# Normalised rows from the ring "in", made by ScalarE alone, and an in-place residual in the channel mixer's second half

## The chip, the cores and the metric

One core of a Trainium2 chip runs the kernel. The metric is the device time of one execution in microseconds (us); the kernel before took 1898.01 us (median of three runs, 1887.8 to 1898.91). Engines are called as in the profile: PE is TensorE (matmuls; PEld its weight loads), DVE is VectorE, ACT is ScalarE, POOL is GpSimd, SP is SyncE. L12 is line 12 of the kernel that the profile belongs to.

## The reference

Two layers of a hybrid backbone over 256 latent and 256 context tokens of 1024 channels. Each layer runs a token mixer and a channel mixer, each on normalised and modulated rows, and each followed by a residual with a second norm:

```python
def _layernorm(x):
    xf = x.astype(F32)
    xc = xf - jnp.mean(xf, axis=-1, keepdims=True)
    var = jnp.mean(xc * xc, axis=-1, keepdims=True)
    return (xc * lax.rsqrt(var + LN_EPS)).astype(x.dtype)

def _modulate(x, shift, scale):
    return _layernorm(x) * (1.0 + scale) + shift

def _post_ln(x, g, b):
    return _layernorm(x) * g + b
...
        x_mid = _post_ln(alpha * x + ada[:, 2] * y, ln1_g[l], ln1_b[l])
...
        h2 = _modulate(x_mid, ada[:, 3], ada[:, 4])
        if l % 2 == 0:
            j = l // 2
            f = _swiglu(h2, ffd_wg[j], ffd_wu[j], ffd_wd[j])
...
        x = _post_ln(alpha * x_mid + ada[:, 5] * f, ln2_g[l], ln2_b[l])
```

The context tokens go through the same steps with a modulation of their own. Matmuls are made of three products of a high and a low part (hi, lo) of each operand.

## The kernel before, in words

The 512 tokens are four tiles of 128 rows; the kernel works on them in two pairs, s = 0 (tiles 0 and 1, the context) and s = 1 (tiles 2 and 3, the latent tokens). A tile of 128 x 1024 numbers is held as two tiles of 128 x 512. These come from rings: "in" has 16, "C" 13 and "B" 14 slots of 128 x 512 (L120), "sg" has 4 (L110); there are three PSUM banks PM for products and three PX for transposes. A slot is given out in the order in which the program asks, and the next tile to take it waits until the last reader of the one before is done. The instructions of each engine are put in order by a scheduler ahead of the run, by priorities and by these rings, so the ring from which a tile comes sets where the instructions on it stand in an engine's order.

The change bears on two places.

Place 1 is the output projection of layer 0, 638 to 705 us. For each pair, `load_x` (L1648) fetches the rows x by POOL's DMA queue into four "in" tiles, `times_alpha` (L1058, ACT) scales them, and `out_proj` runs four groups of 48 matmuls over `tok_group`. `add_residual` takes each group's product: L1039 (DVE) multiplies it by the gate, L1040 (POOL) adds x times alpha, L1041 (DVE) takes the statistics. `post_ln` closes the norm: aggregate (L237), power (L229 DVE, L230 POOL), then the upper half of the columns by ACT and POOL (L1048 nb, L1049, L1050, L1051), the lower half by DVE (L1053, L1054). Then `modulate` calls `normalise`: statistics again (L246), power again, nb (L358), and the normalised rows z of two halves, L360 on ACT and L361 on DVE. PE transposes z in blocks of 128 x 128 (L373) into PX; L379 (DVE, odd blocks) or L381 (ACT, even blocks) applies scale and shift into an sg tile, L382 (ACT) rounds it to its high part, and L383 (DVE) takes the low part. The channel mixer's first matmuls follow (L222 to L224), with their activation at L1107.

Place 2 is the second half of the channel mixer and the start of layer 1's token mixer, 1063 to 1126 us. In `ffn` the down projection is done in halves. In the second, for each pair, four groups of 60 matmuls run, `add_residual` writes into new "in" tiles xn and reads the residual from zs, `post_ln` closes the norm, and `after` saves the latent rows (L1700) and calls `modulate` for layer 1. Behind it in the program stands layer 1's mixer: its first projection with evacuations L528 (ACT) and L531 (DVE), and on POOL a block of memsets and small parameter loads (L541, L547, L466 to L482, L537 to L543) and two loads of a table (L740).

Weights are fetched by SP's queue and split by L215 (ACT, hi) and L216 (DVE, lo) ahead of their matmuls.

Of the kernel before, what the change touches and what calls it, by code (L numbers as in the profile page):

```python
# [14 lines left out]
AF = mybir.ActivationFunctionType  # L15
OP = mybir.AluOpType
# [17 lines left out]
C_ID, C_SEL, _, C_CC, C_SC, C_MF, C_MB, C_ROPE, C_ONE, C_END = (  # L34
    0, 128, 130, 130, 258, 386, 514, 642, 770, 898)
# [60 lines left out]
def hybrid_backbone(ctx: ExitStack, tc: tile.TileContext, A, out, dbg=None, stop=None):  # L96
    nc = tc.nc
# [27 lines left out]
    def tt(tag, dt=F32, n=512):  # L125
        t = S["main"].tile([128, 512], dt, name=tag, tag=tag, bufs=TAGS[tag])
        return t if n == 512 else t[:, :n]
# [16 lines left out]
    def sg():  # L144
        return spool.tile([128, 512], F32, name="sg")
# [96 lines left out]
    def ln_stats(x):  # L242

        st = ln_open(2)
        for i in range(2):
            nc.vector.bn_stats(st[:, i, :], x[i])  # L246
        return ln_close(st)
# [107 lines left out]
    def normalise(x):  # L355
        mu, rs = ln_stats(x)
        nb = cc(1, "nb", bufs=4)
        nc.vector.scalar_tensor_tensor(nb, mu, -1.0, rs, op0=OP.mult, op1=OP.mult)  # L358
        z = [tt("B") for _ in range(2)]
        nc.scalar.activation(z[0], x[0], AF.Identity, scale=rs, bias=nb)  # L360
        nc.vector.tensor_scalar(z[1], x[1], mu, rs, op0=OP.subtract, op1=OP.mult)  # L361
        return z

    def modulate(l, xs, n0, s, act):
# [670 lines left out]

    def add_residual(z, g, p, r, ax, st, quick=False):
        c = slice(256 * (g % 2), 256 * (g % 2) + 256)
        zc = z[g // 2][:, c]
        nc.vector.tensor_tensor(zc, p, r[g // 2][:, c], op=OP.mult)  # L1039
        (nc.vector if quick else nc.gpsimd).tensor_tensor(zc, zc, ax[g // 2][:, c], op=OP.add)  # L1040
        nc.vector.bn_stats(st[:, g, :], zc)  # L1041

    def post_ln(z, st, rows, quick=False):
        g, b = rows
        mu, rs = ln_close(st)
        if not quick:
            nb = cc(1, "nb", bufs=4)
            nc.vector.scalar_tensor_tensor(nb, mu, -1.0, rs, op0=OP.mult, op1=OP.mult)  # L1048
            nc.scalar.activation(z[1], z[1], AF.Identity, scale=rs, bias=nb)  # L1049
            nc.gpsimd.tensor_tensor(z[1], z[1], g[1], op=OP.mult)  # L1050
            nc.gpsimd.tensor_tensor(z[1], z[1], b[1], op=OP.add)  # L1051
        for i in range(2 if quick else 1):
            nc.vector.scalar_tensor_tensor(z[i], z[i], mu, g[i], op0=OP.subtract, op1=OP.mult)  # L1053
            nc.vector.scalar_tensor_tensor(z[i], z[i], rs, b[i], op0=OP.mult, op1=OP.add)  # L1054
# [40 lines left out]
    def ffn(act, xm, fill, plan, after):  # L1095

        wg, wu, wd = A["ffd_wg"][0], A["ffd_wu"][0], A["ffd_wd"][0]
        zs = {}
        hid = {}

        def up(fp, sl):
            sgs = [None, None]

            def ev_g(i, p):
                s = sg()
                sgs[i] = s
                nc.scalar.activation(s[:, sl], p[:, sl], AF.Silu)  # L1107

            def ev_u(i, p):
                s = sgs[i]  # L1110
                nc.vector.tensor_tensor(s[:, sl], s[:, sl], p[:, sl], op=OP.mult)
                if fp + i not in hid:
                    hid[fp + i] = (tt("B", F32R), tt("C", F32R))
                hi, lo = hid[fp + i]
                nc.scalar.activation(hi[:, sl], s[:, sl], AF.Copy)
                nc.vector.tensor_tensor(lo[:, sl], s[:, sl], hi[:, sl], op=OP.subtract)
            col_pair(wg, 128 * fp, act, ev_g, sl)
            col_pair(wu, 128 * fp, act, ev_u, sl)

        def take(at):  # L1120
            for _ in range(plan.count(chr(65 + at))):
                fill.pop(0)()
        for half, (f0, f1) in enumerate(((0, 12), (12, 22))):
            for fp in range(f0, f1, 2):
                if fp == 0:
                    for sl in (slice(0, 256), slice(256, 512)):
                        for f in (0, 2):
                            up(f, sl)
                elif fp > 2:
                    up(fp, slice(0, 512))  # L1130
                if fp == 4:
                    for t in range(4):
                        times_alpha(xm[t])
                take(fp // 2)
            n = f1 - f0
            hh = ([hid[f][0] for f in range(f0, f1)], [hid[f][1] for f in range(f0, f1)])
            if half == 0:
                rows = {j: load_row(S["adarows"][1, 0, j, :], "in") for j in range(2)}
                for t in range(4):
                    zs[t] = xm[t]  # L1140
                for g in range(4):
                    def ev(t, p):
                        c = slice(256 * (g % 2), 256 * (g % 2) + 256)
                        k = sg()[:, :256]
                        nc.vector.tensor_tensor(k, p, rows[0 if t >= 2 else 1][g // 2][:, c], op=OP.mult)
                        nc.gpsimd.tensor_tensor(zs[t][g // 2][:, c], zs[t][g // 2][:, c], k, op=OP.add)
                    tok_group(wd[128 * f0:128 * f1], 256 * g, hh, ev, range(4), kk=n)
                    take(11 + g)
        ln2 = load_row(A["ln2_g"][0], "B"), load_row(A["ln2_b"][0], "B")
        for s in range(2):  # L1150
            tiles = (2 * s, 2 * s + 1)
            st = {t: ln_open(4) for t in tiles}
            xn = {t: [tt("in") for _ in range(2)] for t in tiles}
            for g in range(4):
                tok_group(wd[128 * f0:128 * f1], 256 * g, hh,
                          lambda t, p: add_residual(xn[t], g, p, rows[1 - s], zs[t], st[t]), tiles, kk=n)
                take(15 + 4 * s + g)
            for t in tiles:
                post_ln(xn[t], st[t], ln2)
            after(s, xn)  # L1160

# [488 lines left out]
    with phase("main") as S["main"]:  # L1652
# [24 lines left out]
        with phase("ff") as ff, deeper(ff, 3, 1, 1):  # L1677
            ff.tile([128, 16], F32, name="shift")
            act = new_act()
            rows = load_row(A["ln1_g"][0], "B"), load_row(A["ln1_b"][0], "B")  # L1680
            xm = {}
            for s in range(2):
                ax = {t: times_alpha(load_x(t, nc.gpsimd)) for t in (2 * s, 2 * s + 1)}
# [9 lines left out]
            def after(s, x):  # L1693
                if not act2:
                    act2.extend(new_act())
                for t in x:
                    for i in range(2):
                        dump("x0", x[t][i], lambda o: o[128 * t:128 * t + 128, 512 * i:512 * i + 512])
                        if t >= 2:
                            nc.gpsimd.dma_start(xsave[t - 2, :, 512 * i:512 * i + 512], x[t][i])  # L1700
                modulate(1, x, 0, s, act2)
# [9 lines left out]
        ax = {}  # L1711
# [45 lines left out]
```

## Time and profile before

| | |
|---|---|
| runs, median (lowest to highest) | 1898.01 us (1887.8 to 1898.91) |
| the profiled execution, its own time | 1892.86 us |
| its span, first to last instruction | 1891.1 us |
| mean granted clock of PE | 0.963 |
| busy: PE, DVE, ACT, POOL | 94%, 67%, 44%, 27% of the span |

The profiled execution is one more execution, a little under the median of the others. Start times in the rows count from the start of its span. A row of a timeline shows when it began, for how long its engine was in it, and in brackets how long the engine had been idle before it and what ended that.

### The profile page before, as it was taken

To read this page: it belongs to the slowest core of one execution; us is meant where nothing else is said; L and a number is where in the kernel's file an instruction comes from. 1 tells how busy PE (TensorE), PEld (TensorE's weight loads), DVE (VectorE), ACT (ScalarE), POOL (GpSimd) and SP (SyncE) were. 2 spreads that over 40 slices of the span, in tenths; PEclk is the share of its full clock that TensorE was granted. 3 is DMA by queue.
4 is the path that set the end of the run, shared out by engine and by line. 5 is a ranking of instruction groups with operands and counts; after the bars stand their busy time and mean duration, and the time that the engine had idled before them with its cause. 6 is when DMAs were issued, how large, how long until landed. Compare 5 with 4: busy or idle time off the path is not lost. (4 is left out here: it accounts for less than half of the span.)

```text
span 1891.1 us, 29054 instructions
## 1 busy us (share of the span) xinstructions
PE 1771.9 (94%) x10742; PEld 1408.3 (74%) x10742; DVE 1262.8 (67%) x2063; ACT 828.0 (44%) x1406; POOL 511.4 (27%) x530
## 2 busy tenths in 40 slices
PE   6899989999999979999999989989989899999995
PEld 3777977888777969789788978978979557554831
DVE  5677668666465786767775976587777667754823
ACT  3454555434443464221222445475555255543621
POOL 2353546552112630103101640036513100001000
PEclk8898999999999989999999989999999799999998
DMA  8434421114222636445775644233436789969995
GB/s 306 137 92 129 127 90 45 56 56 128 73 68 89 218 94 212 156 153 160 233 231 179 186 143 123 84 94 97 141 116 214 260 315 393 382 209 392 392 369 202
DMA packets 243933, 337.85 MB, mean 179 GB/s; under 512 B 16008, under 2 KB 158864, under 8 KB 243784
## 3 DMA queue, kind: packets, MB, share of 16 engines
q1 hardware_dynamic: 235896, 318.86, 50.5%
q0 software_dynamic: 6128, 13.96, 2.4%
q10 hardware_dynamic: 1760, 3.09, 0.4%
q8 instruction: 87, 1.43, 0.3%
q14 instruction: 62, 0.51, 0.1%
HBM read 333.74 MB, written 2.12 MB: 178 GB/s over the span
## 5 line engine op out<-in xcount | busy, mean ns | idle before, releaser
L216 DVE TENSOR_TENSOR lo<-raw,hi 128x1024 fp32r<-128x1024 f32 (+1 forms) x370 | 454.6, 1235 | 170.8 <-ACT hi L215 167.8
L215 ACT ACTIVATE hi<-raw 128x1024 fp32r<-128x1024 f32 (+1 forms) x370 | 368.2, 1001 | 439.7 <-PE PM L224 164.6
L222 PE MATMUL PM<-H,hi 128*128 128x512 f32 (+1 forms) x1104 | 388.7, 355 | 6.5 <-ACT sg L1107 2.9
L223 PE MATMUL PM<-H,hi 128*128 128x512 f32 (+1 forms) x1104 | 386.8, 351 | 1.5 <-DVE H L383 1.4
L224 PE MATMUL PM<-H,lo 128*128 128x512 f32 (+1 forms) x1104 | 384.0, 351 | 0.0
L222 PEld LDWEIGHTS PM<-H,hi 128*128 128x128 f32 x1104 | 211.3, 192 | 43.5 <-issue 4.4
L223 PEld LDWEIGHTS PM<-H,hi 128*128 128x128 f32 x1104 | 211.5, 192 | 32.3 <-DVE H L383 2.3
L224 PEld LDWEIGHTS PM<-H,lo 128*128 128x128 f32 x1104 | 210.1, 191 | 31.3 <-issue 2.7
L331 DVE SCALAR_TENSOR_TENSOR ad<-raw,silu,ad 128x512 f32<-128x512 f32 x208 | 176.3, 867 | 33.9 <-issue 12.9
L222 PE MATMUL PM<-hi,H 128*128 128x256 f32 x432 | 127.2, 294 | 4.1 <-ACT in L528 4.1
L223 PE MATMUL PM<-lo,H 128*128 128x256 f32 x432 | 126.8, 294 | 1.9 <-DVE lo L216 1.9
L224 PE MATMUL PM<-hi,H 128*128 128x256 f32 x432 | 125.9, 292 | 0.0
L1023 POOL TENSOR_TENSOR B<-B,sg 128x512 f32<-128x512 f32 (+1 forms) x48 | 62.6, 1316 | 216.5 <-DVE sg L1022 199.7
L1514 POOL TENSOR_TENSOR yl<-sg,yh 128x512 fp32r<-128x512 f32 x17 | 24.3, 1430 | 316.3 <-ACT yh L1513 295.9
L808 POOL TENSOR_TENSOR C<-C,in 128x512 f32<-128x512 f32 (+1 forms) x64 | 82.5, 1313 | 75.0 <-ACT C L807 64.2
L222 PE MATMUL PM<-hi,B 128*128 128x256 f32 x352 | 98.6, 280 | 0.0
L224 PE MATMUL PM<-hi,C 128*128 128x256 f32 x352 | 98.1, 279 | 0.0
L223 PE MATMUL PM<-lo,B 128*128 128x256 f32 x352 | 98.0, 278 | 0.0
L1386 PE MATMUL PM<-raw,xs 128*64 128x512 f32 (+3 forms) x448 | 96.5, 566 | 0.0
L222 PEld LDWEIGHTS PM<-hi,H 128*128 128x128 f32 x432 | 86.3, 200 | 5.7 <-ACT in L528 4.3
L223 PEld LDWEIGHTS PM<-lo,H 128*128 128x128 f32 x432 | 86.4, 200 | 4.1 <-DVE lo L216 2.2
L224 PEld LDWEIGHTS PM<-hi,H 128*128 128x128 f32 x432 | 86.1, 199 | 0.8 <-issue 0.8
(440 smaller groups left out, 3555.8 us busy)
## 6 DMA issues: line engine op xcount, KB each, us to landing
raw<-in_w_ada_dram SPq DMA_DIRECT2D x80, 512.0 KB, 4.3
raw<-in_moe_wd_dram SPq DMA_DIRECT2D x80, 512.0 KB, 8.2
raw<-in_w_gate_dram SPq DMA_DIRECT2D x64, 512.0 KB, 3.7
raw<-in_moe_wg_dram SPq DMA_DIRECT2D x60, 512.0 KB, 8.5
raw<-in_moe_wu_dram SPq DMA_DIRECT2D x60, 512.0 KB, 10.0
raw<-in_w_in_dram SPq DMA_DIRECT2D x54, 512.0 KB, 3.7
raw<-in_ffd_wd_dram SPq DMA_DIRECT2D x28, 512.0 KB, 3.5
raw<-in_ffd_wg_dram SPq DMA_DIRECT2D x26, 512.0 KB, 4.3
```

Source lines behind the costliest of these rows:

```text
L215: nc.scalar.activation(h[:, :m], raw[:, :m], AF.Copy)
L216: (nc.vector if ahead else nc.gpsimd).tensor_tensor(l[:, :m], raw[:, :m], h[:, :m], op=OP.subtract)
L222: nc.tensor.matmul(o, ah, bh, start=start, stop=False, **kw)
L223: nc.tensor.matmul(o, ah, bl, start=False, stop=False, **kw)
L224: nc.tensor.matmul(o, al, bh, start=False, stop=stop, **kw)
L331: nc.vector.scalar_tensor_tensor(acc[j], part, sc, acc[j], op0=OP.mult, op1=OP.add)
L808: nc.gpsimd.tensor_tensor(E[:, xt], E[:, xt], X[:, xt], op=OP.mult)
L1023: nc.gpsimd.tensor_tensor(mixed[c][:, xt], mixed[c][:, xt], s[:, xt], op=OP.add)
L1386: nc.tensor.matmul(po[g, :w.shape[-1]], x[:, c, :], w, start=(c < k), stop=(c + k >= kk), tile_position=(0, g.start))
L1514: nc.gpsimd.tensor_tensor(yl, y, yh, op=OP.subtract)
```

## The change

`normalise` takes z from the ring "in" in place of "B", and ACT makes both halves; L361 on DVE is gone. In the second half of `ffn`, the sum of the residual is written in place into zs; the product of gate and PSUM then goes into half an sg tile, k, and the four "in" tiles xn of each pair are gone. Lines behind the change move by up to two: L1039, L1040 and L1041 become L1041, L1042 and L1043; L1050 and L1051 become L1052 and L1053; L1648 becomes L1649.

```diff
@@ normalise
-        z = [tt("B") for _ in range(2)]
-        nc.scalar.activation(z[0], x[0], AF.Identity, scale=rs, bias=nb)
-        nc.vector.tensor_scalar(z[1], x[1], mu, rs, op0=OP.subtract, op1=OP.mult)
+        z = [tt("in") for _ in range(2)]
+        for i in range(2):
+            nc.scalar.activation(z[i], x[i], AF.Identity, scale=rs, bias=nb)
         return z
@@ add_residual
-        zc = z[g // 2][:, c]
-        nc.vector.tensor_tensor(zc, p, r[g // 2][:, c], op=OP.mult)
-        (nc.vector if quick else nc.gpsimd).tensor_tensor(zc, zc, ax[g // 2][:, c], op=OP.add)
+        zc, k = z[g // 2][:, c], z[g // 2][:, c]
+        if z is ax:
+            k = sg()[:, :256]
+        nc.vector.tensor_tensor(k, p, r[g // 2][:, c], op=OP.mult)
+        (nc.vector if quick else nc.gpsimd).tensor_tensor(zc, k, ax[g // 2][:, c], op=OP.add)
         nc.vector.bn_stats(st[:, g, :], zc)
@@ ffn
-            xn = {t: [tt("in") for _ in range(2)] for t in tiles}
             for g in range(4):
                 tok_group(wd[128 * f0:128 * f1], 256 * g, hh,
-                          lambda t, p: add_residual(xn[t], g, p, rows[1 - s], zs[t], st[t]), tiles, kk=n)
+                          lambda t, p: add_residual(zs[t], g, p, rows[1 - s], zs[t], st[t]), tiles, kk=n)
                 take(15 + 4 * s + g)
             for t in tiles:
-                post_ln(xn[t], st[t], ln2)
-            after(s, xn)
+                post_ln(zs[t], st[t], ln2)
+            after(s, {t: zs[t] for t in tiles})
```

**Place 1 on POOL.** Before, the adds L1040 and the loads of x for the second pair L1648 stood ahead of the first pair's norm L1050, L1051, and adds of the second pair were among it (rs is the power's result):

```order
L1040 TENSOR_TENSOR in<-in 128x256 x4
L1648 DMA in<-in_x_dram 128x512 x4
L1040 TENSOR_TENSOR in<-in 128x256 x4
L230 TENSOR_TENSOR rs<-pwt,mhalf 128x1 x2
L1050 TENSOR_TENSOR in<-in,B 128x512
L1040 TENSOR_TENSOR in<-in 128x256
L1050 TENSOR_TENSOR in<-in,B 128x512
L1040 TENSOR_TENSOR in<-in 128x256
L1051 TENSOR_TENSOR in<-in,B 128x512 x2
L1040 TENSOR_TENSOR in<-in 128x256 x4
L230 TENSOR_TENSOR rs<-pwt,mhalf 128x1 x2
L1040 TENSOR_TENSOR in<-in 128x256 x2
```

After the change the same stretch of POOL reads (lines moved by up to two):

```order
L1042 TENSOR_TENSOR in<-in 128x256 x8
L230 TENSOR_TENSOR rs<-pwt,mhalf 128x1 x2
L1052 TENSOR_TENSOR in<-in,B 128x512 x2
L1053 TENSOR_TENSOR in<-in,B 128x512 x2
L230 TENSOR_TENSOR rs<-pwt,mhalf 128x1 x2
L1649 DMA in<-in_x_dram 128x512 x4
L1042 TENSOR_TENSOR in<-in 128x256 x8
L230 TENSOR_TENSOR rs<-pwt,mhalf 128x1 x2
```

The loads of x moved from ahead of the first pair's last four adds to behind its whole norm and the two powers that its modulation needs, and all eight adds of the second pair stand behind them.

**Place 2 on DVE.** Before, the products of the second pair (L1039) were among the first pair's last steps:

```order
L1039 TENSOR_TENSOR in<-PM,in 128x256 x2
L229 TENSOR_SCALAR pwt<-mv 128x1
L246 BN_STATS bst<-in 128x6
L216 TENSOR_TENSOR lo<-raw,hi 128x1024
L1041 BN_STATS bst<-in 128x6
L237 BN_AGGR mv<-bst 128x2
L1041 BN_STATS bst<-in 128x6
L358 SCALAR_TENSOR_TENSOR nb<-mv,rs 128x1
```

After it, the first products of the second pair, now in sg tiles (L1041), come behind the first pair's modulation (L379, L383):

```order
L216 TENSOR_TENSOR lo<-raw,hi 128x1024
L383 TENSOR_TENSOR H<-sg,H 128x256 x3
L379 TENSOR_SCALAR sg<-PX,adac_120 128x256
L383 TENSOR_TENSOR H<-sg,H 128x256
L379 TENSOR_SCALAR sg<-PX,adac_120 128x256
L1041 TENSOR_TENSOR sg<-PM,in 128x256
L383 TENSOR_TENSOR H<-sg,H 128x256 x3
L1041 TENSOR_TENSOR sg<-PM,in 128x256 x2
L1043 BN_STATS bst<-in 128x6
```

The product of a group frees its PM bank; in the new order the first of them stands behind fifteen or so instructions that begin with the first pair's nb.

**Place 2 on POOL.** Before, the second pair's adds L1040 stood ahead of the block of layer 1, all but two of them, and the table loads L740 came last, behind the rows shown here:

```order
L1051 TENSOR_TENSOR in<-in,B 128x512
L1040 TENSOR_TENSOR in<-in 128x256 x2
L230 TENSOR_TENSOR rs<-pwt,mhalf 128x1 x2
L1040 TENSOR_TENSOR in<-in 128x256 x2
L541 MEMSET H 128x1024
```

After it, six adds stand behind both powers, and L740 is ahead of the block:

```order
L1053 TENSOR_TENSOR in<-in,B 128x512
L230 TENSOR_TENSOR rs<-pwt,mhalf 128x1 x2
L1042 TENSOR_TENSOR in<-sg,in 128x256 x6
L740 DMA B<-in_dft_dram 128x512 x2
L541 MEMSET H 128x1024
```

The last two adds stand behind the block in both orders.

## Rows read from the trace of the kernel before

**Rows 1.** The page's first part: busy us (share of the span) xinstructions.
```profile
PE 1771.9 (94%) x10742; PEld 1408.3 (74%) x10742; DVE 1262.8 (67%) x2063; ACT 828.0 (44%) x1406; POOL 511.4 (27%) x530
```

**Rows 2.** Waits of PE in 640 to 720 us: us in total, times, longest.
```profile
PE PX L373 <- DVE sg L379: 3.3, 2, 2.9
PE PX L373 <- ACT B L360: 2.9, 2, 2.7
```

**Rows 3.** The same view, 1084 to 1145 us.
```profile
PE PX L373 <- ACT B L360: 5.5, 1, 5.5
PE PX L373 <- DVE sg L379: 1.9, 2, 1.1
```

**Rows 4.** Timeline of POOL, place 1: start, us, instruction, count, idle before and releaser.
```profile
638.32 2.15 POOL L1648 DMA_DIRECT2D in<-in_x_dram  x4
...
655.32 1.72 POOL L1040 TENSOR_TENSOR in<-in 128x256 f32<-128x256 f32 x1
...
659.93 3.53 POOL L1051 TENSOR_TENSOR in<-in,B 128x512 f32<-128x512 f32 x2
...
671.84 1.59 POOL L1040 TENSOR_TENSOR in<-in 128x256 f32<-128x256 f32 x2 [0.61 <-DVE in L1039]
```

**Rows 5.** Timeline of DVE, place 1: the last nb.
```profile
689.36 0.16 DVE L358 SCALAR_TENSOR_TENSOR nb<-mv,rs 128x1 f32<-128x1 f32 x1
```

**Rows 6.** Timeline of POOL, place 2.
```profile
1080.57 2.41 POOL L1040 TENSOR_TENSOR in<-in 128x256 f32<-128x256 f32 x2 [0.61 <-DVE in L1039]
1082.93 0.95 POOL L541 MEMSET H<- 128x1024 f32 x1
...
1089.58 2.58 POOL L1040 TENSOR_TENSOR in<-in 128x256 f32<-128x256 f32 x2
1092.14 1.66 POOL L482 TENSOR_SCALAR ng<-ng 128x512 f32<-128x512 f32 x1
1095.70 2.00 POOL L230 TENSOR_TENSOR rs<-pwt,mhalf 128x1 f32<-128x1 f32 x2 [1.91 <-DVE pwt L229]
1098.33 1.28 POOL L1700 DMA_DIRECT2D xsave<-in  x2 [0.62 <-DVE nb L1048]
1099.70 3.59 POOL L1050 TENSOR_TENSOR in<-in,B 128x512 f32<-128x512 f32 x2
1103.25 3.49 POOL L1051 TENSOR_TENSOR in<-in,B 128x512 f32<-128x512 f32 x2
...
1110.44 1.12 POOL L740 DMA_DIRECT2D B<-in_dft_dram  x2
```

**Rows 7.** Timeline of DVE, place 2.
```profile
1080.00 0.16 DVE L358 SCALAR_TENSOR_TENSOR nb<-mv,rs 128x1 f32<-128x1 f32 x1 [0.45 <-POOL rs L230]
...
1085.27 0.53 DVE L379 TENSOR_SCALAR sg<-PX,adac 128x256 f32<-128x256 f32 x1
...
1091.80 1.73 DVE L383 TENSOR_TENSOR H<-sg,H 128x256 fp32r<-128x256 f32 x3
...
1110.68 0.16 DVE L358 SCALAR_TENSOR_TENSOR nb<-mv,rs 128x1 f32<-128x1 f32 x1
```

**Rows 8.** PE in windows of 5 us: width, busy (matmuls), granted clock, DMA, GB/s.
```profile
670.00:675.00 5.00, 1.11 (x6) 0.79 0.66 205
675.00:680.00 5.00, 2.87 (x11) 0.50 0.33 105
680.00:685.00 5.00, 5.00 (x30) 0.68 0.00 0
...
1075.00:1080.00 5.00, 5.00 (x45) 1.00 0.02 3
```

**Rows 9.** Instructions of L360, L361 and L1648: ns min/median/max, or us to landing.
```profile
L360 ACT ACTIVATE B<-in,nb,rs x8: 801/814/817, 670.9 to 1110.9; 128x512 f32<-128x512 f32 x8
...
L361 DVE TENSOR_SCALAR B<-in,mv,rs x8: 525/542/1917, 672.0 to 1110.8; 128x512 f32<-128x512 f32 x8
...
DMA to landing us min/median/max: 2.8/5.4/6.6
```

## The prediction

> **What bounds the kernel now.** I read the busy shares first: PE is busy 94% of a span of 1891.1 us [rows 1], so an instruction less on another engine is worth only what it takes out of PE's gaps. Four times the kernel normalises 128 x 1024 rows for a pair of tiles, in two places: at 638 to 705 us (layer 0's output projection, "place 1") and at 1063 to 1126 us (the channel mixer's second half and the start of layer 1's mixer, "place 2"). The second view was PE's waits there. In place 1 PE's transposes wait 2.9 us for the normalised tiles of L360 and 3.3 us for the modulated tiles of L379 [rows 2]; in place 2 they wait 5.5 and 1.9 us [rows 3]. The third view, the engines' timelines, shows what the normalised tiles themselves waited for. It is neither L360 nor L361, which take 0.81 and 0.54 us [rows 9]; it is the chain in front: residual add on POOL, statistics, power on POOL, norm scale L1050 and L1051 on POOL, statistics again, power again, nb. In place 1 the last residual add ends at 671.84 + 1.59 = 673.43 us [rows 4] and the last nb comes at 689.36 us [rows 5]; in place 2 these are 1089.58 + 2.58 = 1092.16 [rows 6] and 1110.68 us [rows 7]. So POOL's queue, and what stands in it ahead of that last add, decides. That is where the change has to be judged.
>
> **The change, part by part.**
>
> *The eight L361 leave DVE, eight more L360-like rows go to ACT.* DVE is relieved of 8 x 0.54 = 4.3 us (one took 1.92), ACT gets 8 x 0.81 = 6.5 us [rows 9]. DVE's 4.3 us were beside PE's matmuls or beside L360 itself, which took longer, and are worth nothing directly. The price is that the two halves of a tile now follow one another on ACT: up to 0.8 us on each tile, and four in a row for a pair. At the first pair of each place this is hidden (next paragraphs); at the second pair of place 2 I count 1.2 us, since three evacuations of layer 1's first projection (L528, 128 x 256, so an estimate of 0.4 us each, half of L360's 0.81) stand behind these rows on ACT and ahead of the first modulated tile.
>
> Here the Trainium skill speaks against the edit: its page "ScalarE: Activation LUTs", section "Rules for kernel authors", puts additions and multiplications on VectorE, not ScalarE. The traced 0.81 against 0.54 us agrees in direction. If all eight were on the end's path that rule would make 8 x 0.27 = 2.2 us; the order shows that four of them are not.
>
> *The first pair's normalise becomes early, the second pair's input late (place 1).* Tiles of ring "in" are given out in program order, so the x loads of the second pair (L1648), which take "in" tiles after the first pair's z, cannot be issued until that z has its tiles. On POOL the order shows them behind the whole of the first pair's norm. Before, they were issued from 638.32 us [rows 4]. After: two residual adds of 1.72 us no longer stand among L1050 and L1051, so the last L1051, which ended at 659.93 + 3.53 = 663.46 us, ends near 660.0 [rows 4]. Statistics, power and nb behind it took 1110.68 - 1106.74 = 3.9 us at the other place [rows 6, 7], less for the first tile; the loads then issue at about 663.5 to 665.7 us (2.15 us for four [rows 4]), and land 2.8 to 6.6, median 5.4 us later [rows 9]: the first about 669.4, the last about 671.1. The scaling by alpha on ACT follows, and ACT stands there, with the first pair's modulated tiles queued behind it. The eight residual adds of the second pair, of which before six were done by then, all come after 670: at 0.80 us (1.59 for two) to 1.21 us (2.42 for two) [rows 4, 6] they end between 676.4 and 679.7; I take 678.5, 5 us later than 673.43. Part comes back: the first pair's modulation, which filled DVE and ACT in the 15.9 us between that add and the last nb [rows 4, 5], begins earlier, since its normalised tiles are there some 7 us sooner. Nothing given back is +5, all is 0; I take the middle, **+2.5 us**. The two waits of [rows 2] go at the first pair, at best -6.2 us, but only if the second pair isn't late; with loads landing in 6.6 rather than 5.4 us it is +6.2.
>
> *In-place residual, product in an sg tile (place 2).* sg has four tiles, given out in program order: the second pair's eight products k come after the eight modulated tiles hf of the first pair. On DVE the order shows the first two products of the second pair behind the first pair's L383 rows. Three groups of matmuls have then filled the three PM banks, and the last group (60 matmuls) waits for the first bank. When is it freed? The first pair's nb moves from 1080.00 us [rows 7] to about 1073.5 (an estimate: two adds of 1.72 us less in POOL's queue, as in place 1, and about 3 us of the next pair of adds and the idle time in front of the power). Four rows of ACT of 0.81 us [rows 9] behind it make the first L379 possible at about 1077. From the first L379 to the last L383 before, with two splits and two products between, it took 1091.80 + 1.73 - 1085.27 = 8.3 us [rows 7]; the bank is thus free at about 1085.2. The 60 matmuls take 60 x 5/45 = 6.7 us [rows 8] and end at 1091.9. So PE stands for some 4.4 us ahead of them, after the 16 transposes; the 5.5 us wait of [rows 3] belongs to the second pair and is not taken away.
>
> POOL now: the six adds of the second pair begin with the first product, about 1083.5, and at 2.41 us for two [rows 6] end near 1090.7. The two dft loads, which stood at the end (1.12 us at 1110.44), are ahead now, then the fixed block of memsets and parameter loads, 1089.58 - 1082.93 = 6.65 us [rows 6], to 1098.5, and only then the last two adds, which end at 1101: 8.8 us later than 1092.16. The chain to the last nb was 18.5 us. Its POOL rows are 1.66 (L482), 2.00, 1.28, 3.59, 3.49 us, a second pair of saves and of powers, together 14.6 to 15 us [rows 6]; after the change they stand nearly without idle between: last nb about 1115.9, +5.2 us. With the 1.2 us of ACT above the restart of PE's transposes and first modulated tiles is **6.5 us** late. Bounds: -1.9 us if only the wait of [rows 3] on L379 goes and nothing is late; +8.8 + 1.2 = +10 us if nothing comes back.
>
> A second rule of the skill would make it less: the "GPSIMD Engine Reference", section "Key points", says that GpSimd and VectorE share their SBUF interfaces. Two adds took 2.41 us at 1080.57, when DVE was full, and 1.59 at 671.84 [rows 4, 6]; the L361 that fell beside took 1.92 us instead of 0.54 [rows 9], which agrees. By that rule the removed DVE rows would return about 0.8 us, +5.7 for place 2; the products that now crowd there may take it again, and I leave it out.
>
> **Sum.** +2.5 + 6.5 = +9 us. The profiled execution took 1892.86 us, 1.8 around its span; that gives 1901.9. It lies 5.2 us under the median of the runs (1898.01), from which the same sum is 1907.0. I forecast 1904: the change moves the waits rather than removing them. One per cent, 19 us, is about what a measurement of this kernel can tell from no change.
>
> **Rivals.**
>
> *The gain lands (1887 us).* If the x loads and POOL's adds keep pace, the waits of the first pairs go, -6.2 [rows 2] and -1.9 us [rows 3]: 1884.8 by the profiled execution, 1889.9 by the median, 1887 between. For it: the first pair's nb does come 6 to 7 us sooner. Against it: in both places the last add decides, and the order puts more ahead of it. It decides if place 1's loads land within 3 us and the last add ends before 673.5.
>
> *The last group runs at TensorE's lower clock (1917 us).* After a stretch in which PE was busy 1.11 of 5 us, the granted clock was 0.50 in 675 to 680 us, which is 1.2 of 2.4 GHz, and 0.68 in the next [rows 8]; matmuls there lost 0.21 x 1.11 + 0.50 x 2.87 + 0.32 x 5.00 = 3.3 us. The new 4.4 us idle sits right ahead of the last group. If the clock falls, the group ends 3.3 us or, at half clock throughout, 6.7 us later; POOL's memset L541 waits for matmuls of that group, and the last adds stand behind it. Its place is group 3 of the second pair; from 1091.6 us on, when POOL gets there, each us of it is paid in full. Place 2 at +10, the group at +3.3 to 6.7, place 1 at +5 to 6.2 make +18 to 23, with 20.5 about 1913.4 by the profiled execution, 1918.5 by the median. Against it: the 16 transposes just ahead are work too, and it is one gap, where [rows 2] names four.
>
> *Nothing to be seen (1898 us).* What is late at the last add is given back in both places by the emptier DVE. It needs all of the 5 and 8.8 us back, though POOL's own rows are 14.6 us of the 18.5.
>
> **Chances.** Forecast 0.60 (own range 1897 to 1912), gain 0.15, lower clock 0.15, nothing 0.10. Faster than 1879: only if the gain lands with more than I can find, 0.06. Slower than 1917: over half of the lower-clock case and a tail of the forecast, 0.13. Within 1%: 0.81. The range from 1888 to 1921 leaves out about half of the gain case and the upper end of the slow one, some 0.17.
>
> **What would show it.** The changed profile should have: x loads of the second pair at 663 to 666 us; PE's waits for the first pair's normalised tiles gone in both places; a PE wait of about 4 us ahead of the last group of 60 matmuls, released by DVE's products; POOL's last two residual adds of place 2 near 1098 to 1101; the second pair's nb near 1116 instead of 1110.7, the wait for it still there. I am wrong if the last adds end where they did, if PE doesn't stand ahead of the last group, or if the granted clock falls in it.

## The result, and the profile after

The changed kernel took 1910.23 us (median of six runs, 1904.48 to 1916.62), the kernel before 1894.17 us in the same sittings (1887.8 to 1898.91): a ratio of 1.0093, 95% interval 1.0076 to 1.0110. The forecast was 1904 us, slower by 0.3 to 0.5%. So the change is a loss of just under one per cent, small but clear of the spread of the runs. The profiled executions took 1909.78 and 1892.86 us, 16.9 us apart.

Where do the 16.9 us come from? PE runs 10,742 matmuls in both kernels, so the start of the n-th matmul in one execution can be set against that in the other. The table has the difference (after minus before) at the end of each stretch and what the stretch added to it:

| stretch, time in the kernel before | matmul | difference at its end, us | added, us | forecast |
|---|---|---|---|---|
| up to the first difference of the programs, 637 us | 3400th | -2.5 | -2.5 | 0 |
| place 1, to 705 us | 3800th | +1.8 | +4.3 | +2.5 |
| the channel mixer, to 1070 us | 6000th | +1.2 | -0.6 | 0 |
| place 2, to 1134 us | 6400th | +11.1 | +9.9 | +6.5 |
| layer 1's mixer, to 1556 us | 9200th | +13.8 | +2.6 | 0 |
| the experts of layer 1, to 1837 us | 10600th | +16.8 | +3.1 | 0 |

Up to 637 us the two programs are the same, and yet 2.5 us apart: so much do two executions differ by themselves. In the channel mixer between the two places, 365 us that PE fills, they differ by 0.6 us more.

PE's waits in place 1, 640 to 720 us of the kernel after, as in [rows 2] (engine and line, waited for: us in total, times, longest):

```profile
PE PX L373 <- ACT in L361: 5.2, 3, 2.5
PE PM L223 <- DVE H L383: 5.0, 4, 1.7
```

L373 is PE's transpose of the normalised rows z; L361 now makes both halves of z on ACT. Of the 5.2 us, 1.45 (at 662.4 us) are still the first pair's, where before all were; 2.48 and 1.30 us (at 691.9 and 694.1) are for the second pair's z. The wait wasn't removed, most of it moved to the other pair. POOL's timeline there answers to [rows 4]:

```profile
660.73 1.07 POOL L230 TENSOR_TENSOR rs<-pwt,mhalf 128x1 f32<-128x1 f32 x2 [1.90 <-DVE pwt L229]
661.75 2.19 POOL L1649 DMA_DIRECT2D in<-in_x_dram  x4
668.08 2.12 POOL L1042 TENSOR_TENSOR in<-in 128x256 f32<-128x256 f32 x3 [4.15 <-ACT in L1060]
670.37 4.66 POOL L1042 TENSOR_TENSOR in<-in 128x256 f32<-128x256 f32 x5 [0.17 <-DVE in L1041]
678.35 1.00 POOL L230 TENSOR_TENSOR rs<-pwt,mhalf 128x1 f32<-128x1 f32 x1 [3.33 <-DVE pwt L229]
```

This execution was 2.5 us ahead when it came here, so for comparison 2.5 us belong on these times. The loads of x are issued at 661.75 (664.2), where 663.5 was forecast; the last add ends at 675.03 (677.5), where 678.5 was. The last nb (minus mean times rs, which L361 needs) comes at 692.99 us (695.5) on DVE, 6.1 us later than in [rows 5]:

```profile
692.99 0.16 DVE L358 SCALAR_TENSOR_TENSOR nb<-mv,rs 128x1 f32<-128x1 f32 x1 [0.44 <-POOL rs L230]
```

In place 2, 1063 to 1150 us, PE waits as follows, to be read against [rows 3]:

```profile
PE PX L373 <- ACT in L361: 9.4, 3, 7.9
PE PM L222 <- DVE sg L1041: 4.0, 1, 4.0
```

The 4.0 us are the wait ahead of the last group that was forecast at 4.4. POOL's timeline answers to [rows 6]:

```profile
1086.41 4.96 POOL L1042 TENSOR_TENSOR in<-sg,in 128x256 f32<-128x256 f32 x6 [9.59 <-DVE sg L1041]
1091.38 1.18 POOL L740 DMA_DIRECT2D B<-in_dft_dram  x2
1092.57 0.96 POOL L541 MEMSET H<- 128x1024 f32 x1
...
1099.05 2.10 POOL L1042 TENSOR_TENSOR in<-sg,in 128x256 f32<-128x256 f32 x2
...
1105.44 0.57 POOL L230 TENSOR_TENSOR rs<-pwt,mhalf 128x1 f32<-128x1 f32 x1 [1.84 <-DVE pwt L229]
1109.68 0.65 POOL L1701 DMA_DIRECT2D xsave<-in  x1 [3.68 <-DVE pwt L229]
```

POOL stands for 9.6 us until the first product in sg, then does six adds, the table loads and the block, and ends the last add at 1101.15 us. This execution was 1.2 us behind when it came to place 2, so that is 1099.9 in the time of before, 7.8 us later than there; 8.8 were forecast. What was not forecast stands in the last two rows: POOL then waits twice, 1.84 and 3.68 us, for DVE. The first wait is for pwt, the statistics' last step. The second is that of the save L1701, which stands ahead of the second power and reads a half tile that DVE's norm (L1056) finished at 1109.39 us; the profile names the second pwt, which was done 0.06 us later. DVE's timeline shows why both were late:

```profile
1100.44 1.80 DVE L216 TENSOR_TENSOR lo<-raw,hi 128x1024 fp32r<-128x1024 f32 x1 [0.58 <-ACT hi L215]
1103.16 1.23 DVE L216 TENSOR_TENSOR lo<-raw,hi 128x1024 fp32r<-128x1024 f32 x1 [0.92 <-ACT hi L215]
1104.30 0.42 DVE L1043 BATCH_NORM_STATS2 bst<-in 128x6 f32<-128x256 f32 x1
...
1109.31 0.14 DVE L229 TENSOR_SCALAR pwt<-mv 128x1 f32<-128x1 f32 x1
...
1120.72 0.16 DVE L358 SCALAR_TENSOR_TENSOR nb<-mv,rs 128x1 f32<-128x1 f32 x1 [0.68 <-POOL rs L230]
```

The sum that the statistics L1043 need was ready at 1101.15, but two weight splits L216 of layer 1's mixer stand ahead of them, and those wait for ACT's L215, which in turn waits for PE to be through with the matmuls ahead (and so to free a weight tile):

```profile
1099.35 1.06 ACT L215 ACTIVATE hi<-raw 128x1024 fp32r<-128x1024 f32 x1 [1.56 <-PE PM L223]
1102.07 1.06 ACT L215 ACTIVATE hi<-raw 128x1024 fp32r<-128x1024 f32 x1 [1.66 <-PE PM L223]
```

The last nb comes at 1120.72 (1119.5), 8.8 us later than in [rows 7]; 5.2 were forecast.

The clock, 5 us windows of PE as in [rows 8]:

```profile
1080.00:1085.00 5.00, 1.97 (x10) 0.95 0.39 109
1085.00:1090.00 5.00, 2.28 (x10) 0.50 0.35 102
1090.00:1095.00 5.00, 5.00 (x40) 0.86 0.33 105
```

After the idle ahead of the last group the granted clock fell to 0.50 (1.2 of 2.4 GHz), as the slower rival had it. The group of 60 matmuls ran from 1087.72 to 1096.69 us, 9.0 us where 6.7 were reckoned.

At last a place where nothing was expected, layer 1's mixer. Between its 7200th and 7300th matmul the changed kernel loses 2.7 us. PE's waits in that stretch before (1242.5 to 1262.7 us):

```profile
PE PM L222 <- ACT sg L1012: 2.4, 1, 2.4
PE PB L753 <- ACT B L748: 1.6, 1, 1.6
PE PM L222 <- ACT B L501: 0.6, 1, 0.6
PE PM L223 <- DVE B L502: 0.5, 1, 0.5
```

and after (1253.6 to 1276.5 us):

```profile
PE PM L222 <- ACT B L501: 3.5, 1, 3.5
PE PB L753 <- ACT B L748: 1.6, 1, 1.6
PE PX L814 <- POOL C L808: 1.4, 1, 1.4
```

No edited line is near, but the scheduler put the same instructions in another order there. The waits are 1.4 us longer in sum, and the mean granted clock of the stretch is 0.85 where it was 0.92; how the 2.7 us divide between the two was not separated.

### The profile page after: what moved, and what is told of

It reads as the page before. It is cut to its first block, busy times and chain, and to the rows that moved or that the text cites. A ratio compares the mean times of both kernels' runs of the same rounds, so it can differ in the third digit from the quotient of the medians.

```text
span 1908.0 us, 29057 instructions
## 1 busy us (share of the span) xinstructions
PE 1770.3 (93%) x10742; PEld 1402.6 (74%) x10742; DVE 1257.9 (66%) x2055; ACT 832.7 (44%) x1414; POOL 509.2 (27%) x530
## 5 line engine op out<-in xcount | busy, mean ns | idle before, releaser
L216 DVE TENSOR_TENSOR lo<-raw,hi 128x1024 fp32r<-128x1024 f32 (+1 forms) x370 | 451.4, 1227 | 183.7 <-ACT hi L215 182.1
L215 ACT ACTIVATE hi<-raw 128x1024 fp32r<-128x1024 f32 (+1 forms) x370 | 367.5, 1000 | 440.6 <-PE PM L224 160.4
L222 PE MATMUL PM<-H,hi 128*128 128x512 f32 (+1 forms) x1104 | 388.8, 355 | 8.2 <-ACT sg L1109 2.8
L224 PE MATMUL PM<-H,lo 128*128 128x512 f32 (+1 forms) x1104 | 384.8, 351 | 0.0
L222 PEld LDWEIGHTS PM<-H,hi 128*128 128x128 f32 x1104 | 211.1, 192 | 46.3 <-issue 4.4
L224 PEld LDWEIGHTS PM<-H,lo 128*128 128x128 f32 x1104 | 211.2, 192 | 31.7 <-issue 2.7
L222 PE MATMUL PM<-hi,H 128*128 128x256 f32 x432 | 125.7, 291 | 4.1 <-ACT in L528 4.1
L224 PE MATMUL PM<-hi,H 128*128 128x256 f32 x432 | 124.8, 289 | 0.0
L222 PE MATMUL PM<-hi,B 128*128 128x256 f32 x352 | 99.4, 282 | 4.0 <-DVE sg L1041 4.0
L224 PE MATMUL PM<-hi,C 128*128 128x256 f32 x352 | 98.6, 280 | 0.0
L222 PEld LDWEIGHTS PM<-hi,H 128*128 128x128 f32 x432 | 85.0, 197 | 5.6 <-ACT in L528 4.3
L224 PEld LDWEIGHTS PM<-hi,H 128*128 128x128 f32 x432 | 85.0, 197 | 0.8 <-issue 0.8
```

The costliest lines, as they stand in the source:

```text
L215: nc.scalar.activation(h[:, :m], raw[:, :m], AF.Copy)
L216: (nc.vector if ahead else nc.gpsimd).tensor_tensor(l[:, :m], raw[:, :m], h[:, :m], op=OP.subtract)
L222: nc.tensor.matmul(o, ah, bh, start=start, stop=False, **kw)
L224: nc.tensor.matmul(o, al, bh, start=False, stop=stop, **kw)
```

## Experiments

Each of them was timed against the kernel before, whose medians in these sittings were 1890.6 to 1894.7 us, so the ratios are what to compare, not the medians. The table gives the median, the ratio with its interval, and from the profiled execution what place 1 (3400th to 3800th matmul), place 2 (6000th to 7000th, a later end because some orders move a few matmuls over the earlier one) and layer 1's mixer behind it (7000th to 9200th) added to the kernel before.

| kernel | median us | ratio | place 1 | place 2 | mixer 1 |
|---|---|---|---|---|---|
| the change | 1910.23 | 1.0093 (1.0076 to 1.0110) | +4.3 | +9.9 | +2.6 |
| act_only | 1896.94 | 1.0031 (1.0013 to 1.0049) | +1.2 | -3.1 | +5.0 |
| z_only | 1914.01 | 1.0101 (1.0061 to 1.0141) | +6.0 | +5.4 | +5.5 |
| k_in_c | 1903.96 | 1.0066 (1.0042 to 1.0089) | +3.9 | +6.0 | +0.8 |
| x_early | 1910.33 | 1.0098 (1.0077 to 1.0120) | +2.0 | +13.1 | +5.4 |
| place1_b | 1913.72 | 1.0109 (1.0075 to 1.0143) | +1.3 | +13.2 | +2.4 |
| stats_first | 1907.10 | 1.0083 (1.0054 to 1.0112) | +4.4 | +13.4 | +1.7 |
| block_late | 1910.67 | 1.0095 (1.0060 to 1.0131) | +4.8 | +13.2 | -1.6 |
| second_in_b | 1910.55 | 1.0084 (1.0051 to 1.0118) | +4.5 | +11.5 | +3.8 |
| k_c_both | 1899.35 | 1.0042 (1.0028 to 1.0056) | +4.6 | +2.6 | +1.2 |
| before_both | 1897.55 | 1.0030 (1.0012 to 1.0048) | +0.5 | +5.3 | -0.8 |
| best1 | 1897.19 | 1.0015 (0.9998 to 1.0032) | +1.4 | +1.3 | +4.9 |

How far to trust a single column: six kernels besides the change have its order in place 1 (z_only, k_in_c, stats_first, block_late, second_in_b, k_c_both), and cost 3.9 to 6.0 us there, so place 1 is known to about 1 us, once to 2. In place 2, x_early and place1_b have the order of the change but for a few instructions (DVE's evacuation L531, a copy out of PSUM, now ahead of an aggregation L237; the first L1052 on POOL ahead of the second power), and gave 13.1 and 13.2 against 9.9. The three are within 0.2 us of one another up to the 6250th matmul, and x_early and place1_b within 0.1 us at the end, so the 3 us look like the price of the moved instructions and not like chance. For the other kernels the side effects of an edit on the order weren't separated: up to 3 us in place 2 can be one. In layer 1's mixer seven kernels (the change, act_only, z_only, x_early, place1_b, second_in_b, best1) lose the same 2.7 us between the 7200th and the 7300th matmul, and k_in_c, block_late and k_c_both lose nothing there; the rest of that column, -0.3 to 2.8 us over the seven, comes later.

**act_only: the kernel before, both halves by ScalarE, z still from ring B.**

```diff
         z = [tt("B") for _ in range(2)]
-        nc.scalar.activation(z[0], x[0], AF.Identity, scale=rs, bias=nb)
-        nc.vector.tensor_scalar(z[1], x[1], mu, rs, op0=OP.subtract, op1=OP.mult)
+        for i in range(2):
+            nc.scalar.activation(z[i], x[i], AF.Identity, scale=rs, bias=nb)
```

> The kernel before with both halves of the normalised rows made by ScalarE, z still from ring B. Theory (the lateness comes from the order that the rings give): 1894 us as before, within 3 us, since B's order is kept; the second halves cost up to 0.8 us at each of the two second pairs. Rival (ScalarE's serial halves carry the cost): at least a third of the 16 us, 1900 us or more.

The time rose by 0.31%, some 6 us of 1890.6, against "within 3": as much as the rival expected, "a third of the 16 us", though not for the rival's reason. The places of the edit themselves cost +1.2 and -3.1 us, so ScalarE's serial halves are cheap; the -3.1 come with another order of the splits on DVE, so it isn't shown that they are the halves' own. The loss is +5.0 us in layer 1's mixer, 2.7 of them from the order that appears in the kernel after too: PE's matmuls of the mixer stand in the same order in both. Here it comes without any change of ring.

**z_only: z from "in" and by ScalarE, the residual not in place.**

```diff
-        z = [tt("B") for _ in range(2)]
-        nc.scalar.activation(z[0], x[0], AF.Identity, scale=rs, bias=nb)
-        nc.vector.tensor_scalar(z[1], x[1], mu, rs, op0=OP.subtract, op1=OP.mult)
+        z = [tt("in") for _ in range(2)]
+        for i in range(2):
+            nc.scalar.activation(z[i], x[i], AF.Identity, scale=rs, bias=nb)
```

> The kernel before with z from ring in and by ScalarE; the residual of the second half still goes to tiles of its own, not in place. Theory: place 1 costs the same 4.3 us as in the whole change, place 2 less than half of its 9.9 us because the products do not wait for the first pair's modulation: 1900 us (1897 to 1904). Rival (the ring of z alone makes all of it): 1908 to 1912 us with PE's wait of about 4 us ahead of the last group still there.

A miss: 1914 us, as slow as the whole change (three of its four runs took 1913 to 1916 us, one 1901). Neither story fits as it stood. Place 2 does cost less, +5.4 us, and PE's wait ahead of the last group is gone, so the rival's mark is missing; but place 1 cost 6.0 and layer 1's mixer 5.5 us. The ring of z, with ScalarE's halves, suffices to be late, and POOL's timeline in place 2 shows with what:

```profile
1100.50 1.43 POOL L1040 TENSOR_TENSOR in<-in 128x256 f32<-128x256 f32 x2
...
1112.30 1.73 POOL L230 TENSOR_TENSOR rs<-pwt,mhalf 128x1 f32<-128x1 f32 x2 [8.88 <-DVE pwt L229]
```

The power waits 8.9 us for pwt after the last add. In [rows 6] that idle time was 1.9 us.

**k_in_c: the change with the product in ring C.**

```diff
-            k = sg()[:, :256]
+            k = tt("C")[:, :256]
```

> The changed kernel with the product k from ring C, which has three free tiles, instead of sg. Theory: the products are made before the first pair's modulation, PE's 4.0 us wait ahead of the last group goes, place 2 comes back to within 3 us of before: 1900 us (1896 to 1904). Rival (the order of sg is not the cause, POOL's fixed block is): the last adds end no earlier than in the changed kernel, 1908 to 1911 us.

PE's waits in place 2, 1063 to 1150 us:

```profile
PE PX L373 <- ACT in L361: 10.6, 3, 9.6
PE PM L222 <- DVE v L531: 2.4, 1, 2.4
```

and POOL behind the last add:

```profile
1091.12 1.44 POOL L1042 TENSOR_TENSOR in<-C,in 128x256 f32<-128x256 f32 x2
...
1099.74 1.00 POOL L230 TENSOR_TENSOR rs<-pwt,mhalf 128x1 f32<-128x1 f32 x1 [5.69 <-DVE pwt L229]
```

The wait ahead of the last group is gone and the last add ends at 1092.56 us, 0.4 us from [rows 6], so sg's order was what the prediction said it was: it made the products and with them the group and the add late. But of the 9.9 us only about 4 came back, so the theory's "within 3 us of before" failed: place 2 is still 6.0 us late, and the time of 1904 is at the edge of what was expected. The last add is where it was in the kernel before, but the power now waits 5.7 us for DVE, where it waited 1.9. So the last add doesn't decide alone.

**x_early and place1_b: place 1.** The first asks for all x ahead of the first projection, the second takes z from B in place 1 (here and below `normalise` gets the ring as an argument; the diff shows what it comes to).

```diff
+            xr = {t: load_x(t, nc.gpsimd) for t in range(4)}
             for s in range(2):
-                ax = {t: times_alpha(load_x(t, nc.gpsimd)) for t in (2 * s, 2 * s + 1)}
+                ax = {t: times_alpha(xr[t]) for t in (2 * s, 2 * s + 1)}
```

> The changed kernel with the loads of x for the second pair asked for ahead of the first pair's projection. Theory: place 1's 4.3 us go or turn to a gain of up to 3 us, place 2 stays: 1905 us (1902 to 1907). Rival (the loads landed in time anyway, and place 1's cost is the order of POOL's adds behind both powers): place 1 changes by less than 1.5 us, 1909 to 1911 us.

```diff
-        z = [tt("in") for _ in range(2)]
+        z = [tt("B" if l == 0 else "in") for _ in range(2)]
```

> The changed kernel with ring B for z in place 1 only, made by ScalarE alone as in the changed kernel. Theory (in place 1 the ring makes the loads of x and the second pair's adds late): place 1 costs 0 to 2 us instead of 4.3, as in the kernel with ScalarE alone (1.2 us), place 2 stays at about 10 us, 1906 us. Rival (the serial halves on ScalarE make place 1 late): 3.5 us or more in place 1, 1909 to 1911 us.

Place 1 falls to +2.0 and +1.3 us, the total of neither does, since place 2 came out 3 us dearer in both. From these two and act_only, place 1's 4.3 us are about: 1.2 for the serial halves on ScalarE (1.2 and 1.3 with ring B) and 2.3 for the late loads of x (x_early against the change). The 0.8 left could be the adds that the order keeps behind both powers, but they are within the accuracy of the column. The rival of x_early expected less than 1.5 us from the loads, and the theory all of 4.3; both are off.

**stats_first and block_late: what holds place 2 in the change.** stats_first queues the splits of layer 1's mixer, from the third on, behind the second pair's last pwt; block_late queues the block of memsets and loads on POOL behind the second pair's last power (the same lines for the three other issues of the block). Shown are the lines that set the order; those that count the splits and remember the two instructions are left out.

```diff
@@ split_w: stats_first
+            if S.get("held") is not None and S["nsplit"] > S["held"]:
+                st.enter_context(tc.issue_after(S["hold"].ins))
             (nc.vector if ahead else nc.gpsimd).tensor_tensor(l[:, :m], raw[:, :m], h[:, :m], op=OP.subtract)
@@ mixer: block_late
+            with (tc.issue_after(pw_last.ins) if L1 else ExitStack()):
-            nc.gpsimd.memset(rawm, 0.0)
+                nc.gpsimd.memset(rawm, 0.0)
```

> The changed kernel with the weight splits of layer 1's mixer, from the third on, queued on VectorE behind the second pair's last pwt (the input of the power). Theory (the statistics stood behind splits that PE paces): the first power after the last add comes within 2.5 us of it instead of 4.3, the second right behind; place 2 costs 5 to 7 us instead of 9.9, 1906 us. Rival (only the end of the last add decides, as predicted): no more than 1 us gained, 1909 to 1911 us.

> The changed kernel with layer 1's block of memsets and parameter loads on GpSimd queued behind the second pair's last power. Theory (the block holds the last two adds only as long as the last group of matmuls does not): the last adds end 2 us earlier, near 1099 instead of 1101.2 us, since the last products came at 1097.6, and 1908 us. Rival (the block is what makes the last add late, as the prediction's sum had it): the last adds end 5 us or more earlier, 1904 us or less.

In stats_first the statistics do come first: both powers run at 1102.2 us, 1.5 us behind the last add and without idle time between. And yet place 2 isn't cheaper. PE's waits show what is late in their place:

```profile
PE PM L225 <- DVE v L534: 6.2, 1, 6.2
PE PM L225 <- DVE sg L1044: 4.0, 1, 4.0
```

(lines are 3 higher than in the change.) The 8 us wait for z became a wait of 6.2 us for v L534, an evacuation on DVE that now stands behind the norm, and PE has it ahead of the transposes. What held L534 is the split in front of it, which took 5.72 us where the usual one takes 1.2, and ended as POOL's rows of the norm and its saves did:

```profile
1109.01 5.72 DVE L219 TENSOR_TENSOR lo<-raw,hi 128x1024 fp32r<-128x1024 f32 x1
1114.65 0.74 DVE L534 COPY v<-PM 128x256 f32<-128x256 f32 x2
```

```profile
1109.94 1.27 POOL L1056 TENSOR_TENSOR in<-in,B 128x512 f32<-128x512 f32 x1
1111.16 2.48 POOL L1057 TENSOR_TENSOR in<-in,B 128x512 f32<-128x512 f32 x2
1113.58 1.12 POOL L1705 DMA_DIRECT2D xsave<-in  x2
```

So the theory was right that the powers come sooner and wrong on the worth. How much the order alone would give back, with that split elsewhere, was not tried.

In block_late the rival falls, and so does the theory's gain in time: of the 2 us expected at the adds one came, and place 2 cost no less. The last two adds wait for their products, not for the block:

```profile
1088.45 4.96 POOL L1046 TENSOR_TENSOR in<-sg,in 128x256 f32<-128x256 f32 x6 [9.59 <-DVE sg L1045]
1099.76 2.43 POOL L1046 TENSOR_TENSOR in<-sg,in 128x256 f32<-128x256 f32 x2 [6.35 <-DVE sg L1045]
```

This execution was 2.0 us behind the change's when it came to place 2, so the adds end 1 us earlier than there. Block and last group are late together, and to take one away leaves the other. That the group is this late is in part the lower clock; how the place would go with a fast group wasn't tried.

**second_in_b: z of the second pair from B.** In the change, layer 1's first evacuations L528, which take "in" tiles, run after the second pair's z.

```diff
-        z = [tt("in") for _ in range(2)]
+        z = [tt("B" if s else "in") for _ in range(2)]
```

> The changed kernel with the normalised rows of the second pair taken from ring B again (both pairs of calls), the first pair's from in. Theory (layer 1's first evacuations L528 take in tiles, so with z in the same ring they stand behind the second pair's z, and PE runs out of PM banks): L528 runs ahead of the second pair's z again, PE's wait of 8 us for z shrinks by 2 to 4 us, place 2 costs 6 to 8 us instead of 9.9, place 1 is as in the changed kernel, 1907 us. Rival (only the products in sg and the block on GpSimd count): place 2 costs 9 to 11 us, 1909 to 1912 us.

L528 runs at 1099 to 1111 us now, ahead of z at 1117.7, as intended, and place 2 costs 11.5 us: within the spread of the change's order, 9.9 to 13.2, and a little above the rival's 9 to 11. While the products are late, this order is hidden behind them.

**k_c_both, before_both and best1: mended versions.** k_c_both is k_in_c with both rules of order; before_both is the kernel before with them; best1 is the change with k from C and z from "in" in one call only, the first pair's in place 2:

```diff
-            k = sg()[:, :256]
+            k = tt("C")[:, :256]
@@ normalise
-        z = [tt("in") for _ in range(2)]
+        z = [tt("B" if s or l == 0 else "in") for _ in range(2)]
```

> The changed kernel with the products from ring C, layer 1's block behind the last power and the splits behind the last pwt. Theory (three orders make place 2 late, each of them mended here): last adds end near 1087 us, second pair's nb near 1106, place 2 gains 3 to 6 us against before where the change lost 9.9; place 1 keeps its 4 us: 1891 us (1887 to 1896). Rival (the serial halves on ScalarE, or the wait of mixer 1 on its weights, sets the end of place 2): 1899 us or more.

> The kernel before with the same two rules of order: layer 1's block behind the last power, splits behind the last pwt. Theory (the last add stood behind the block for 6.65 us, so this helps the kernel before as well): last adds end near 1086 instead of 1092.2 us, 4 to 6 us gained, 1886 us. Rival (what is moved behind is late next, at layer 1's parameters): within 2 us of before.

> The change kept only where nothing stands behind the ring: z from in for the first pair of place 2 alone, from B elsewhere, the product k from C. Theory (three orders, not the moved work, make the change slow): place 1 costs about 1 us, place 2 between -2 and 3 us, layer 1's mixer 1 to 6 us with the order that the scheduler finds: 1895 us (1890 to 1900). Rival (writing in place or ScalarE's serial halves cost 5 us or more by themselves): 1903 us or more.

before_both is the plainest miss, and the most useful. Its last add of place 2 is early, as meant:

```profile
1078.58 2.40 POOL L1047 TENSOR_TENSOR in<-in 128x256 f32<-128x256 f32 x2 [2.45 <-DVE in L1046]
1084.52 2.19 POOL L233 TENSOR_TENSOR rs<-pwt,mhalf 128x1 f32<-128x1 f32 x2 [3.54 <-DVE pwt L232]
```

It ends at 1080.98 us in an execution that was 6.9 us ahead, so 4.3 us earlier than in [rows 6], and yet place 2 ended 5.3 us later. PE's waits (L225 to L227 and L219 are L222 to L224 and L216 of the kernel before):

```profile
PE PM L225 <- ACT hi L215: 6.2, 2, 5.8
PE PM L226 <- DVE lo L219: 3.0, 2, 1.9
PE PM L227 <- DVE lo L219: 2.1, 1, 2.1
```

The splits that were put behind the statistics are layer 1's weights, and PE needs them now. The last add got earlier, and the work with which PE had covered the norm came later. Here too a split stood beside POOL's rows of the norm, 4.00 us from 1092.20. k_c_both has the same kind of waits, 5.4 us for splits beside 7.5 for the norm; its place 2 cost 2.6 us where the theory had 3 to 6 gained, and its 1899 us are the rival's. best1 without the two rules came in as expected: it costs 1.4 and 1.3 us in the two places and isn't to be told from the kernel before (1.0015, 0.9998 to 1.0032); of its 4.9 us in layer 1's mixer 2.7 are the order found there. With k in C, place 2 costs 4.7 us less when z of the second pair is from B (6.0 in k_in_c, 1.3 here; the ring in place 1 differs too), where with k in sg that was worth nothing. No version beat the kernel before.

## Why the prediction was right, and where it wasn't

The direction, the two places and the main waits held: the waits were moved, not removed, and the measured time is within the range. The size did not hold. The sum had +9 us for the two places; the trace has 4.3 + 9.9 = 14.2 us there, and 16.9 over the whole kernel. That 1910 us still lies near 1904 is in part luck: the range is wide, and the kernel before came out at 1894.17 us, 3.8 under the 1898.01 that the forecast took as its upper base, which hides part of the miss. Nor is one per cent about what can be told from no change here: the interval of the ratio is 0.0034 wide. Of the three signs of being wrong that the prediction named, one appeared, the lower clock in the last group. Point by point:

- *ScalarE's halves are cheap.* Right as far as shown: act_only cost +1.2 and -3.1 us in the two places, the second with another order on DVE. That its total rose by 0.31% has another cause, layer 1's mixer.
- *x loads behind the first pair's norm.* Right to a microsecond: issue 664.2 against 663.5, last add 677.5 against 678.5 us, by the clock of before. The step that failed is the one behind them, "part comes back ... I take the middle, +2.5 us". Nothing came back: 4.1 us late at the add, 4.3 at the end. PE's wait for the first pair's z, which should have gone, was still 1.45 us. The power after the last add waited 3.3 us for pwt, as it had waited 2.96 us before; DVE's relief wasn't in that stretch. Of the 4.3 us the x loads are only about half, by x_early.
- *sg's order.* Right: PE waits 4.0 us ahead of the last group, released by L1041, and k_in_c takes this away.
- *Last add at 1101, 8.8 us late.* It ended at 1099.9 by the clock of before, 7.8 us late. Right in size, partly because two errors cancel: the first add came at 1086.41 (1085.2), not at 1083.5, and the six adds then took 4.96 us, where 2.41 for two would make 7.2. And too simple in cause: the add waits for the block and for the group alike (block_late).
- *The chain behind it, "nearly without idle", last nb +5.2.* Wrong, +8.8: from the last add to the last nb it took 19.6 us, where 18.5 were read before and 14.9 were reckoned (the rows it adds up make 14.4). POOL stood 1.84 and 3.68 us for DVE, since the scheduler had put weight splits that PE paces ahead of the statistics. This is the mis-sized term of place 2: 9.9 against 6.5 us.
- *The clock.* The prediction made it a rival, at 0.15, and a sign of being wrong. It did fall in the last group, to 0.50, and the group took 9.0 instead of 6.7 us: 2.3 us, where the rival had 3.3 to 6.7. So its event came and its 1917 us didn't. Of its price the add shows little: the memset L541 followed the table loads without a wait, and the adds followed the block. What it costs by way of the splits, which start once the group is through (ACT's L215 stood 8.86 us until 1095.31), wasn't separated, so part of the chain's lateness may be the clock's.
- *The slow L361.* The prediction reads its 1.92 us as an effect of the two adds beside it. Only the end of the second add ran beside it (1082.65 to 1082.98 us); from there on it was the memsets from L541 on.
- *Layer 1's mixer.* Not foreseen, +2.6 us. The order was read at two places only, and it changes at a third, 130 us behind the last edit.

Still open: the 3.1 us in the experts of layer 1 (0.0 to 4.7 over the kernels tried), and which edit turns the order in layer 1's mixer: act_only has it with no ring changed, best1 has it, k_in_c doesn't. How place 2 would go with the clock kept at 1.00 in the last group wasn't tried either.

In-place writing with z in ring B and the product in sg was not run. From the program, z would wait there for slots that only the last group frees, and that group for a PM bank, which the products in sg free only behind the modulation of that z; no run shows this.

## What to carry to other kernels

Where tiles are given out in program order, the ring of a tile is an order of work: before an operand is moved to another ring, list who asks that ring for tiles next (here the loads of x, the evacuations of the next stage, the products in sg) and what stands behind them on their engines. A chain that runs over three in-order queues isn't set by its last big step; read for each hop what stands ahead of it, above all instructions paced by the engine that the chain feeds. An instruction moved out of the way lands beside others: read its duration there, too. And where a scheduler decides, compare the orders over the whole program, since an edit can turn the order in a stage that it doesn't touch.

## What the hardware showed that was not expected

A split on DVE that runs beside POOL can take far longer than usual. In the kernel before, 271 of the 310 splits of 128 x 1024 took 1.20 to 1.48 us, with POOL's computing rows beside them for 15% of that time; the other 39 took 1.50 to 2.32 us, with POOL beside them for 77%. The longest ones came where an edit had put a split beside POOL's rows of the norm: 5.72 us in stats_first and 4.00 in before_both. POOL beside a split isn't enough by itself: 38 of the 271 had it for over half their time.

That ScalarE making both halves left place 2 faster by 3.1 us than the halves shared with VectorE (act_only) was not expected from 0.81 against 0.54 us; the L361 that took 1.92 us beside the end of an add and POOL's memsets [rows 9] is gone there, and the splits on DVE are in another order, and neither was measured by itself. And the granted clock fell to 0.50 in 1085 to 1090 us after 1.97 us of PE work in the 5 us before, all of it transposes (ten).
